# Hybrid attention layer on one core: background transfers without their marks, the heads' values fetched later, the latents' squares three tiles later

## The chip, the core and the metric

The kernel runs on one core of a Trainium2 chip. The core has five engines with instruction streams of their own, which meet only at semaphores: PE (TensorE, matmuls, with its weight loads shown apart as PEld), DVE (VectorE), ACT (ScalarE), POOL (GpSimd) and SP (SyncE). In this kernel SP issues nearly all plain transfers, POOL issues the transfers that add to their target and some stores, and all of them are carried out by the core's 16 DMA engines. The metric is the device time of one execution in microseconds (us), the median over several executions. A measurement of this kernel can tell a change of about 0.5% from none.

## The reference

One decoder layer on 512 tokens of width 2048. The input is normalised and projected; one half of the heads are latent attention heads (MLA, with a rotary part), the other half "forgetting" heads (FoX, whose logits get a running sum of log forget gates). Both are gated, joined, projected back, normalised and added to the input.

```python
def _hybrid_layer(x, cos, sin, g_pre, w_in, g_q, w_uq, g_kv, w_ukv, b_forget, w_out, g_post):
    h = _rms_norm(x, g_pre)
    proj = h @ w_in
    split_points = np.cumsum(IN_SPLITS)[:-1].tolist()
    (q_lat, kv_lat, k_rope_raw, gate_mla,
     fq, fk, fv, f_logit, gate_fox) = jnp.split(proj, split_points, axis=-1)
    o_mla = _mla_branch(q_lat, kv_lat, k_rope_raw, g_q, w_uq, g_kv, w_ukv, cos, sin) * jax.nn.silu(gate_mla)
    o_fox = _fox_branch(fq, fk, fv, f_logit, b_forget) * jax.nn.silu(gate_fox)
    o = jnp.concatenate([o_mla, o_fox], axis=-1) @ w_out
    return x + _rms_norm(o, g_post)
```

Attention is causal, with 8 heads of each kind and 128 columns to a head. Everything is float32.

## The kernel before

**Numbers and matmuls.** Every float32 operand is divided into a high part (a cast on ACT) and a low part (a subtraction on DVE); a product is three matmuls, high by high, high by low and low by high (`mm3`, L148 to L151). Weights come in chunks of 512 KB. `load` issues a chunk's transfer on SP into a tile `raw` (L239 for blocks and sums, L256 for plain columns, L247 for a second addend); `divide` makes `whi` (ACT, L276) and `wlo` (DVE, L279) of it; PE then uses the chunk. `chunk(i)` loads four chunks ahead and divides two ahead. A `raw` tile is one of a few buffers, so a load waits until an earlier chunk's `wlo` is done.

**Stages.** From the start to about 45 us: transposes of x and the first narrow projection (`proj_first`). To 230 us: the value projection `v` and two pairs of FoX gates, in turns with the first q and k. To 420 us: four FoX head pairs (loop at L1253), each a q (`fox_q`), a k (`fox_k`), scores and values. To 600 us: latents (`l`) and MLA gates (`m`). To 725 us: four MLA head pairs. Then the output projection.

**Fewer products, more sums.** The products `v`, `l`, `m` and the output use a scheme of the Strassen-Winograd kind: seven products of half blocks in place of eight, for which blocks of weights are added to or taken from each other first. Some of these sums of weights are made by the DMA engines in the background, through DRAM, and they are the subject here. The list `bg` has 36 of them: `t7` and `t6` for each of `v`, `l` and `m` (four blocks each, 512 KB a block), and `t7`, `t6` and `t4` for the output `o` (four blocks each, 1024 KB a block). A sum takes two transfers: a *first*, a plain copy of one weight block from DRAM to DRAM on SP (L312), and an *accumulate* of the other addend on POOL (L309). The accumulate of a `t6` has the finished `t7` for its addend, that of a `t4` the finished `t6`.

**Steps and marks.** `paced` counts the tiles that PE has been given. Whenever as many have gone by as the pace says (`set_pace`: 4 at first, then 20, 8, 12, 4.9 and so on; double for a wide block), it calls `add_step(n)`, which stands in the program for: the accumulate of sum n-1, the first of sum n, and a *mark* for sum n+1 (L314). The mark is a transfer of 64 bytes on SP, from the `whi` tile that PE is about to use to the first row of the target of sum n+1. The first of sum n+1 overwrites the same bytes, so it must wait for the mark to land, and the mark must wait for the cast of that `whi`. The counter starts at -1, so that sum 0 gets a mark as well.

**Order.** Nothing but a small part at the start is ordered by hand. A planner lists the instructions of each engine; in that list an instruction may stand ahead of one that comes earlier in the program, where the earlier one has something to wait for. Each engine then runs its list strictly in order, and a wait of one holds all behind it. A few instructions are kept in program order (`in_order`).

**Small steps between tiles.** `todo` is a list of small steps. `pump(rate)` runs `rate` of them after each tile of a product, `wait(n)` puts n empty ones in, `drain` runs what is left. Scores, values, divisions of activations and latents all go through it. Of these, three are touched:
- `load_v` (L1130) fetches one head pair's values from DRAM (`v_away`, put there by POOL at the end of the `v` stage) on SP (L1133); `split_v` (L1136) divides them. Before, the fetch stands ahead of the pair's q, and the division ahead of the values of the pair before (for the first pair: at the end of its scores).
- `wait(4)` (L1250) stands ahead of the first pair's scores.
- `latent(i)` (L1306 the square on ACT, L1310 the sum on DVE) for the first four latents, in the product `g5` of `l`, and for the next four in the product `q6` of `m`; the first four read what `lat_less` (L1380) has just written. `lat_sum` is L1376.

Of the kernel before, what the change touches and what calls it, by code (L numbers as in the profile page):

```python
# [12 lines left out]
F32 = mybir.dt.float32  # L13
# [6 lines left out]
P = 128  # L20
D = 2048
S = 512
NT = S // P
# [42 lines left out]
def tile_hybrid_layer(  # L66
# [32 lines left out]
    def slot(name, dt=F32, shape=(P, 2, S)):  # L99

        return sp.tile(list(shape), dt, tag="s", name=name)
# [177 lines left out]
        dve.tensor_tensor(out=lo[:, :m], in0=raw[:, :m], in1=hi[:, :m].bitcast(F32), op=ALU.subtract)  # L279
        ready[i] = [t[:, :m].rearrange("p (k c) -> p k c", k=n) for t in (hi, lo)]  # L280

    state = {"loaded": 0, "divided": 0, "tiles": 0, "step": -1, "pace": 4}

    def prepare(i):
        while state["divided"] < min(len(chunks), i + 1):
# [15 lines left out]
    W, made = {}, {}  # L301
    bg = []

    def add_step(n, mark):


        if n > 0:
            to, _, second = bg[n - 1]
            pool.dma_start(to.rearrange("p (k c) -> p k c", k=2), second, accum_op=ALU.add)  # L309
        if 0 <= n < len(bg):  # L310
            to, first, _ = bg[n]
            nc.sync.dma_start(to.rearrange("p (k c) -> p k c", k=2), first)  # L312
        if n + 1 < len(bg):
            nc.sync.dma_start(bg[n + 1][0][0:1, 0:16], mark)  # L314

    def sum_blocks(g, block, late, width=512):

# [201 lines left out]
    def wait(n):  # L519
        todo.extend([lambda: None] * n)  # L520
# [5 lines left out]
    def set_pace(n):  # L526
        state.update(pace=n, tiles=0)

    def paced(w):

        if state["step"] <= len(bg):
            state["tiles"] += 1
            wide = 0 <= state["step"] < len(bg) and bg[state["step"]][0].shape[1] > 1024
            pace = state["pace"] * (1 + wide)
            if state["tiles"] >= pace:
                state["tiles"] -= pace
                add_step(state["step"], w[0:1, 0, 0:16].bitcast(F32))
                state["step"] += 1

    def proj_T(rng, outs, kh, kl, rate=1):  # L540

        k = 0
        n_k = sum(chunks[i][3] for i in rng)
        for i in rng:
            hi, lo = chunk(i)
            for j in range(chunks[i][3]):
                for o, rows, pick in outs:
                    mm3(o[:rows, :], pick(hi, j), pick(lo, j), kh[k], kl[k], k == 0, k == n_k - 1)
                k += 1
                pump(rate)  # L550
                paced(hi)

    def piece_of(banks, t, width):

# [132 lines left out]
    def enqueue_values(hs):  # L687
        steps = [(h, kb) for h in hs for kb in range(NT)]
        for i in range(len(steps) + 1):
            if i < len(steps):  # L690
                h, kb = steps[i]
                todo.append(lambda h=h, kb=kb: h.flip(kb))
            if i > 0:
                h, kb = steps[i - 1]
                todo.append(lambda h=h, kb=kb: h.values(kb))
# [294 lines left out]
    def product(name, g, parts, o, first, last, rate=1, at=None, held=0, side=(), turned=False):  # L990


        side = deque(side)
        kk = 0

        def step(j, kk, t, hi, lo):
            if not turned:
                mm3(
                    o[t], *parts(kk, t), hi[:, j, :], lo[:, j, :], first and kk == 0, last and kk == 7,
                    skip_group_check=True,  # L1000
                )
                return
            for f in range(2):
                c = slice((2 * t + f) * P, (2 * t + f + 1) * P)
                mm3(
                    o[t][:, f * HALF : (f + 1) * HALF], hi[:, j, c], lo[:, j, c], *parts(kk),
                    first and kk == 0 and f == 0, last and kk == 7, skip_group_check=True,
                )

        rng = list(prods[name, g])  # L1010
        for i in rng[: len(rng) - held]:
            hi, lo = chunk(i)
            for j in range(2):
                if at is not None and kk == at[0]:
                    at[1]()
                for t in range(2):
                    step(j, kk, t, hi, lo)
                kk += 1
                pump(rate)
                paced(hi)  # L1020
                if side and not held and kk % 2 == 0:
                    side.popleft()()
        w = [chunk(i, ahead=0) for i in rng[len(rng) - held :]]
        if w:
            side.popleft()()
        for t in range(2):
            for m in range(2 * len(w)):
                step(m % 2, kk + m, t, *w[m // 2])
            if w:
                finish(t, 2, o[t])  # L1030
# [31 lines left out]
    def fox_k(p, wholes):  # L1062
        kb = [proj_bank(f"fk{p}{i}") for i in range(2)]
        proj_T(fox[p]["k"], [(kb[i], P, two[i]) for i in range(2)], hh, hl)
        k = []
        for i in range(2):
            t = tmp(f"fkt{p}{i}")
            dve.tensor_tensor(out=t, in0=kb[i], in1=rrow, op=ALU.mult)
            k.append(split(t, f"fk{p}{i}"))
            whole_block(wholes, 2 + i, t)  # L1070
        return k
# [55 lines left out]
        for t in range(2):  # L1127
            act.mul(to[:, t, :], o[t], col[:, t0 + t : t0 + t + 1])

    def load_v(pair):  # L1130

        both = slot(f"fv{pair}", shape=(P, NT, 256))
        nc.sync.dma_start(both, v_away[pair].rearrange("p (t c) -> p t c", t=NT))  # L1133
        return both

    def split_v(pair, both):  # L1136

        tiles = v_pair(f"fv{pair}")
        return lambda: values_into(tiles, slice(0, 256), [both[:, t, :] for t in range(NT)], True)
# [107 lines left out]
    v_room.close()  # L1247
    pp = heads_room.enter_context(tc.tile_pool(name="pp", bufs=2, reuse_waits="tile"))
    set_pace(4.9)
    wait(4)  # L1250

    heads = None
    for p in range(4):  # L1253
        vt = load_v(3 - p)
        if p:
            q, wholes = fox_q(p)
            drain()
            keys = [load_keys(2 * (3 - p) + i) for i in range(2)]
            todo.append(split_v(3 - p, vt))
            enqueue_values(heads)  # L1260
            k = fox_k(p, wholes)
            keys = [forget_keys(*a) for a in keys]
            drain()
        else:
            keys = [forget_keys(*a) for a in keys]
            later = split_v(3, vt)
        if p == 2:
            nc.sync.dma_start(gains2[0:6, :], g_q.rearrange("o (k p) -> (o k) p", p=P))
            nc.sync.dma_start(gains2[6:10, :], g_kv.rearrange("o (k p) -> (o k) p", p=P))
            make_gcol(gains2, NK, 10)  # L1270
        vs = values_of(f"fv{3 - p}")
        heads = []
        for i in range(2):
            h = 2 * (3 - p) + i
            heads.append(
                Head(
                    f"f{h}", [q[i]], [k[i]],
                    vs[i],
                    lambda h=h: gates[h],
                    [tuple(wholes[:, 0, c * P : (c + 1) * P] for c in (i, 2 + i))], keys[i],  # L1280
                )
            )
        enqueue_scores(heads, 1)
        if p == 0:
            todo.append(later)
    l4 = slot("l4b", shape=(P, NT, L4))
    nc.sync.dma_start(l4, l4_away.rearrange("p (t c) -> p t c", t=NT))
# [80 lines left out]
    def lat_block(f, half):  # L1368
        return [raws_of[1 + 2 * f + t][:, :, half * HALF : (half + 1) * HALF] for t in range(2)]
# [4 lines left out]
    def lat_sum(to, o, add, op=ALU.add):  # L1374
        for t in range(2):
            dve.tensor_tensor(out=to[t], in0=fold(o[t]), in1=add[t], op=op)  # L1376

    def lat_less(to, o):
        for t in range(2):
            dve.tensor_tensor(out=to[t], in0=to[t], in1=fold(o[t]), op=ALU.subtract)  # L1380
# [65 lines left out]
    product("g7", "l", sums_wide("g7"), C, False, True, side=[*f3[2:], *d3[:2]], turned=True)  # L1446
    lat_sum(lat_block(1, 1), C, pl, ALU.subtract)
    lat_less(lat_block(0, 1), C)
    for i in range(4):
        todo.append(lambda i=i: latent(i, raw(i)))  # L1450
    G = [proj_bank(f"gdl{t}") for t in range(2)]
# [1 line left out]
    lat_sum(lat_block(1, 1), G, lat_block(1, 1))  # L1453
    product("g3", "l", sums_wide("g3"), G, False, True, turned=True)
    lat_sum(lat_block(1, 0), G, lat_block(1, 0))
    for i in range(4, 8):
        todo.append(lambda i=i: latent(i, raw(i)))
    wait(2)
    todo.append(lambda: latent_stats(1))
    for i in range(6):  # L1460
        todo.append(lambda i=i: latent_part(i))
# [29 lines left out]
    for p in range(4):  # L1491
# [31 lines left out]
        for i in c["kv"]:  # L1523
            hi, lo = chunk(i)
            for j in range(chunks[i][3]):
                fst, lst = kk == 0, kk == KVR // P - 1
                for n in range(2):
                    w = cols(256 * n)
                    mm3(kb[n], w(hi, j), w(lo, j), knh[kk], knl[kk], fst, lst)
                for t in range(NT):  # L1530
                    o = vb[t // 2][:, (t % 2) * 256 : (t % 2) * 256 + 256]
                    ts = slice(t * P, (t + 1) * P)
                    mm3(
                        o, knh[kk][:, ts], knl[kk][:, ts], v_cols(hi, j), v_cols(lo, j),
                        fst and t % 2 == 0, lst, skip_group_check=True,
                    )
                kk += 1
                pump(2)
                paced(hi)
        k = [[split(kb[i], f"mk{p}{i}"), (kr, None)] for i in range(2)]  # L1540
        kw = [[whole_block(wholes, 2 + i, kb[i]), kr.bitcast(F32)[:, :P]] for i in range(2)]
        drain()
# [231 lines left out]
```

## Time and profile before

| What | Value |
|---|---|
| Times of three runs | 902.98, 903.35 and 906.58 us, median 903.35 us |
| Profiled execution | 903.03 us, of which the span from the first instruction to the last is 901.3 us |
| Granted TensorE clock | 0.997 of full speed |
| PE busy | 885.5 us |
| DVE, ACT and POOL busy | 678.0, 454.2 and 66.0 us |
| Moved by the DMA engines | 218.26 MB, mean 242 GB/s |

The profile is one execution. A matmul of 512 columns is shown as some 390 ns long but the next one starts after some 230 ns, since they are pipelined; so a busy share of PE near 100% says that it was never without work, not that nothing could go faster. In the views, "SPq" is the transfer queue of SP, a bracket after a row gives the idle time of the engine ahead of the instruction and what ended it, and "xN" counts instructions.

### The profile page before, as it was taken

To read this page: it belongs to the slowest core of one execution; us is meant where nothing else is said; L and a number is where in the kernel's file an instruction comes from. 1 tells how busy PE (TensorE), PEld (TensorE's weight loads), DVE (VectorE), ACT (ScalarE), POOL (GpSimd) and SP (SyncE) were. 2 spreads that over 40 slices of the span, in tenths; PEclk is the share of its full clock that TensorE was granted. 3 is DMA by queue.
4 is the path that set the end of the run, shared out by engine and by line. 5 is a ranking of instruction groups with operands and counts; after the bars stand their busy time and mean duration, and the time that the engine had idled before them with its cause. 6 is when DMAs were issued, how large, how long until landed. Compare 5 with 4: busy or idle time off the path is not lost.

```text
span 901.3 us, 12830 instructions
## 1 busy us (share of the span) xinstructions
PE 885.5 (98%) x4594; PEld 755.4 (84%) x4594; DVE 678.0 (75%) x1120; ACT 454.2 (50%) x837; POOL 66.0 (7%) x86
## 2 busy tenths in 40 slices
PE   8999999999999999999999999999999999999997
PEld 8988887888878888888998998788888888877885
DVE  4579995658775738667588897867978895988786
ACT  6944443334243423435545565535554676646383
POOL 1010110011211101000000000000000000000021
PEclk9999999999999999999999999999999999999998
DMA  9798799799999999896799986788862136799878
GB/s 288 229 267 241 223 317 304 223 238 305 259 282 279 243 244 240 212 271 153 276 398 393 331 293 169 152 211 196 220 149 79 62 119 212 232 324 306 278 214 253
DMA packets 125515, 218.26 MB, mean 242 GB/s; under 512 B 16362, under 2 KB 53764, under 8 KB 124428
## 3 DMA queue, kind: packets, MB, share of 16 engines
q1 hardware_dynamic: 113340, 179.41, 61.0%
q0 software_dynamic: 11376, 37.75, 21.0%
q8 instruction: 36, 0.59, 0.3%
q10 hardware_dynamic: 736, 0.29, 0.1%
q14 instruction: 27, 0.22, 0.1%
HBM read 202.72 MB, written 65.03 MB: 297 GB/s over the span
## 4 chain that ended last, share of the span: by engine, by line
PE 74%; DVE 14%; DMA 6%; issue 3%; ACT 3%; SPq 0%; ACTq 0%; DVEq 0%
DVE wlo L279 4%; PE in L583 3%; PE fk L151 3%; PE fk L149 3%; PE fk L150 3%; PE fq L149 3%; PE fq L151 3%; PE fq L150 3%; PE sm L626 2%; PE mq L149 2%; PE mq L151 2%; PE mq L150 2%; ACT whi L276 1%; PE oa L149 1%; PE od L150 1%
## 5 line engine op out<-in xcount | busy, mean ns | idle before, releaser
L279 DVE TENSOR_TENSOR wlo<-raw,whi 128x1024 fp32r<-128x1024 f32 (+3 forms) x217 | 256.7, 1187 | 128.9 <-ACT whi L276 119.7
L276 ACT CAST whi<-raw 128x1024 fp32r<-128x1024 f32 (+3 forms) x217 | 221.2, 1023 | 256.8 <-issue 34.8
L149 PE MATMUL fk<-h,whi 128*128 128x512 f32 x128 | 52.4, 410 | 0.0
L149 PE MATMUL fq<-h,whi 128*128 128x512 f32 x128 | 50.8, 397 | 0.0
L149 PE MATMUL fg<-h,whi 128*128 128x512 f32 x128 | 50.3, 393 | 0.0
L151 PE MATMUL fk<-h,wlo 128*128 128x512 f32 x128 | 50.2, 392 | 0.0
L150 PE MATMUL fk<-h,whi 128*128 128x512 f32 x128 | 50.1, 391 | 0.0
L151 PE MATMUL fq<-h,wlo 128*128 128x512 f32 x128 | 50.0, 390 | 0.0
L150 PE MATMUL fq<-h,whi 128*128 128x512 f32 x128 | 49.9, 390 | 0.0
L151 PE MATMUL fg<-h,wlo 128*128 128x512 f32 x128 | 49.9, 390 | 0.0
L150 PE MATMUL fg<-h,whi 128*128 128x512 f32 x128 | 49.9, 390 | 0.0
L266 DVE TENSOR_TENSOR raw<-raw,second 128x1024 f32<-128x1024 f32 x32 | 39.0, 1217 | 0.8 <-DMA second<-in_w_out_dram 0.8
L648 ACT ACTIVATE pf<-sf,stf 128x128 f32<-128x128 f32 (+3 forms) x32 | 16.7, 523 | 30.0 <-DVE stf L641 30.0
L583 PE MATMUL in<-whi,h 128*128 128x328 f32 x128 | 29.7, 321 | 0.0
L149 PE MATMUL mq<-ln,whi 128*128 128x512 f32 x72 | 28.8, 400 | 0.0
L151 PEld LDWEIGHTS fk<-h,wlo 128*128 128x128 f32 x128 | 24.0, 188 | 5.3
L151 PEld LDWEIGHTS fq<-h,wlo 128*128 128x128 f32 x128 | 24.0, 188 | 5.3
L151 PEld LDWEIGHTS fg<-h,wlo 128*128 128x128 f32 x128 | 24.0, 188 | 5.1
L150 PE MATMUL mq<-ln,whi 128*128 128x512 f32 x72 | 28.3, 392 | 0.0
L151 PE MATMUL mq<-ln,wlo 128*128 128x512 f32 x72 | 28.2, 391 | 0.0
L150 PEld LDWEIGHTS fg<-h,whi 128*128 128x128 f32 x128 | 24.1, 188 | 4.7
L149 PEld LDWEIGHTS fg<-h,whi 128*128 128x128 f32 x128 | 24.0, 188 | 4.7
(558 smaller groups left out, 2465.4 us busy)
## 6 DMA issues: line engine op xcount, KB each, us to landing
raw<-in_w_in_dram SPq DMA_DIRECT2D x96, 512.0 KB
raw<-in_w_out_dram SPq DMA_DIRECT2D x32, 512.0 KB
second<-in_w_in_dram SPq DMA_DIRECT2D x24, 512.0 KB
bmg<-awaymg SPq DMA_DIRECT2D x20, 256.0 KB
awaymg<-rmg POOLq DMA_DIRECT2D x8, 512.0 KB, 7.9
raw<-t6v SPq DMA_DIRECT2D x8, 512.0 KB
t7o<-in_w_out_dram SPq DMA_DIRECT2D x4, 1024.0 KB
t7o<-in_w_out_dram POOLq DMA_DIRECT2D x4, 1024.0 KB, 10.5
```

The lines of the kernel that those rows point to most:

```text
L149: pe.matmul(o, ah, bh, start=first, stop=False, **kw)
L150: pe.matmul(o, ah, bl, start=False, stop=False, **kw)
L151: pe.matmul(o, al, bh, start=False, stop=last, **kw)
L266: tc.keep_in_program_order(dve.tensor_tensor(out=raw, in0=raw, in1=second, op=ALU.add))
L276: cast = act.copy(hi[:, :m], raw[:, :m])
L279: dve.tensor_tensor(out=lo[:, :m], in0=raw[:, :m], in1=hi[:, :m].bitcast(F32), op=ALU.subtract)
L583: pe.matmul(banks[t][:, :n], a[k][:, tss[t]], b[:, j, :], start=k == 0 and m == 0, stop=k == NK - 1 and m == 2,)
L626: pe.matmul(s[:, :nn], a[:, qs], c[:, :nn], start=(i == 0), stop=(i == len(pairs) - 1))
L648: act.activation(p, s[:, :n], AF.Exp, bias=st[:, 0:1], scale=unit, accum_out=st[:, 1:2])
```

## The change

The marks go: `add_step` no longer issues them, `paced` no longer hands a tile over, and the counter starts at 0. The values of the first FoX pair are fetched by a step placed twelfth in the list that runs in the next q; those of the others are fetched after the pair's q and keys and divided after the values of the pair before. The four empty steps ahead of the first scores become two. Three empty steps are put ahead of each group of four latents, and the two ahead of `latent_stats(1)` become one.

```diff
-    state = {"loaded": 0, "divided": 0, "tiles": 0, "step": -1, "pace": 4}
+    state = {"loaded": 0, "divided": 0, "tiles": 0, "step": 0, "pace": 4}
...
-    def add_step(n, mark):
+    def add_step(n):
...
         if 0 <= n < len(bg):
             to, first, _ = bg[n]
             nc.sync.dma_start(to.rearrange("p (k c) -> p k c", k=2), first)
-        if n + 1 < len(bg):
-            nc.sync.dma_start(bg[n + 1][0][0:1, 0:16], mark)
...
-    def paced(w):
+    def paced():
...
-                add_step(state["step"], w[0:1, 0, 0:16].bitcast(F32))
+                add_step(state["step"])
...
-    def load_v(pair):
+    def load_v(pair, both=None):
-        both = slot(f"fv{pair}", shape=(P, NT, 256))
+        both = both or slot(f"fv{pair}", shape=(P, NT, 256))
...
     set_pace(4.9)
-    wait(4)
+    wait(2)
     heads = None
     for p in range(4):
-        vt = load_v(3 - p)
         if p:
             q, wholes = fox_q(p)
             drain()
             keys = [load_keys(2 * (3 - p) + i) for i in range(2)]
-            todo.append(split_v(3 - p, vt))
+            vt = load_v(3 - p)
             enqueue_values(heads)
+            todo.insert(10, split_v(3 - p, vt))
             k = fox_k(p, wholes)
...
         else:
             keys = [forget_keys(*a) for a in keys]
-            later = split_v(3, vt)
+            first_v = slot("fv3", shape=(P, NT, 256))
+            later = split_v(3, first_v)
...
         enqueue_scores(heads, 1)
         if p == 0:
+            todo.insert(12, lambda: load_v(3, first_v))
             todo.append(later)
...
     lat_less(lat_block(0, 1), C)
+    wait(3)
     for i in range(4):
         todo.append(lambda i=i: latent(i, raw(i)))
...
     lat_sum(lat_block(1, 0), G, lat_block(1, 0))
+    wait(3)
     for i in range(4, 8):
         todo.append(lambda i=i: latent(i, raw(i)))
-    wait(2)
+    wait(1)
     todo.append(lambda: latent_stats(1))
```

More of the change, by code (lines that the diff above doesn't have):

```diff
@@ L550, in proj_T @@
                 pump(rate)
-                paced(hi)
+                paced()
     def piece_of(banks, t, width):
@@ L1019, in product @@
                 pump(rate)
-                paced(hi)
+                paced()
                 if side and not held and kk % 2 == 0:
@@ L1538, in tile_hybrid_layer @@
                 pump(2)
-                paced(hi)
+                paced()
         k = [[split(kb[i], f"mk{p}{i}"), (kr, None)] for i in range(2)]
```

## The prediction

> **What bounds the kernel now.** I read the page first, then what PE waits for, then the transfer queue of SP in order of time. The profiled execution took 903.03 us: the span below and 1.7 us around it. It stands 0.3 us under the median of the three runs, 903.35 us, so its terms can be set against that median as they are. A measurement of this kernel tells about 0.5%, 4.5 us, from no change.
>
> ```profile
> span 901.3 us, 12830 instructions
> ...
> PE 885.5 (98%) x4594; PEld 755.4 (84%) x4594; DVE 678.0 (75%) x1120; ACT 454.2 (50%) x837; POOL 66.0 (7%) x86
> ```
>
> PE is without work for 901.3 - 885.5 = 15.8 us in all. The four waits that this change could reach are in the view of waits, PE alone:
>
> ```profile
> PE sm L626 <- ACT pm L648: 1.3, 1, 1.3
> ...
> PE gdl L149 <- DVE lat L1376: 1.1, 1, 1.1
> PE ptf L657 <- ACT pf L648: 1.1, 1, 1.1
> ...
> PE sf L626 <- ACT pf L648: 0.4, 1, 0.4
> ```
>
> Each is a single wait, 3.9 us together. So whatever the edits do for PE's waits is worth at most 3.9 us, and the question is what they may break: PE's feed. How full the DMA engines are that feed it is in the view of windows (the last two columns are their busy share and GB/s; the second stretch holds little but one 1024 KB first, the third little but its accumulate):
>
> ```profile
> 45.00:230.00 185.00, 184.14 (x815) 151.58 (x814) 142.96 (x184) 77.96 (x98) 20.83 (x25) 1.00 0.90 263
> 562.00:566.00 4.00, 3.90 (x18) 2.77 (x16) 3.89 (x10) 0.91 (x4) 0.00 (x0) 1.00 0.66 151
> 568.00:576.00 8.00, 7.38 (x31) 5.30 (x30) 7.29 (x15) 5.46 (x8) 0.00 (x0) 1.00 0.97 171
> ```
>
> From 45 to 230 us they are busy for 0.90 of the time; 0.10 x 185 = 18.5 us is free. At full share a first moves 151 / 0.66 = 229 GB/s, an accumulate 171 / 0.97 = 176 GB/s.
>
> **The marks: what holds a first in its place?** The planner may put a transfer ahead of earlier ones that have to wait. SP's queue shows how far this goes:
>
> ```profile
> 19.50 0.95 SPq L247 DMA_DIRECT2D second<-in_w_in_dram  x2
> 20.49 0.36 SPq L1268 DMA_DIRECT2D gains<-in_g_q_latent_dram  x1
> 21.68 0.27 SPq L1269 DMA_DIRECT2D gains<-in_g_kv_latent_dram  x1
> ```
>
> L1268 and L1269 stand in the third round of the loop over FoX pairs, work that PE reaches after 300 us. They read an input, wait for nothing of their stage, and go out at 20 us, when SP's earlier loads have to wait for buffers. The `second` loads belong to the first chunks that have two addends, whose own `raw` loads, the first of line L239, go out at 105.71 us (below). And a first leaves when its own mark allows it, not when its step comes:
>
> ```profile
> 105.71 3.31 SPq L239 DMA_DIRECT2D raw<-in_w_in_dram  x2
> 109.08 0.32 SPq L314 DMA_DIRECT2D t6v<-whi  x1
> 111.33 0.37 SPq L239 DMA_DIRECT2D raw<-in_w_in_dram  x1
> 112.19 0.57 SPq L312 DMA_DIRECT2D t6v<-in_w_in_dram  x1
> ...
> 141.35 0.28 SPq L314 DMA_DIRECT2D t7v<-whi  x1
> ```
>
> In the program the first at 112.19 stands directly ahead of the mark at 141.35, one whole step behind its own mark at 109.08. It went 3 us behind its own mark, past the loads between. A first reads weights and writes a DRAM tile of its own; without the mark it waits for nothing. I therefore expect all 36 firsts to move to where the `gains` went, about 17 to 45 us, at 0.57 us of issue each, 36 x 0.57 = 20.5 us, ahead of or between the loads that PE needs from 30 us on. By the trace of before, how many were out by 230 us (all instructions of line L312 in that window):
>
> ```profile
> L312 SPq DMA_DIRECT2D t7v<-in_w_in_dram x4: 564/708/1312, 41.8 to 145.1; - x4
> L312 SPq DMA_DIRECT2D t6v<-in_w_in_dram x4: 563/566/568, 46.2 to 150.6; - x4
> L312 SPq DMA_DIRECT2D t7l<-in_w_in_dram x3: 563/573/1324, 173.6 to 226.5; - x3
> L312 SPq DMA_DIRECT2D t6l<-in_w_in_dram x2: 564/564/564, 179.9 to 213.7; - x2
> ```
>
> Thirteen. Moved forward are 23: 11 of 512 KB and 12 of 1024 KB, 17.5 MiB or 18.35 MB. At 229 GB/s that is **80 us** of all DMA engines, of which 18.5 us fall into free time: **+61.5 us**, if the accumulates all stayed where they are. They won't all: each can go once its first has landed. Before, 12 are issued by 230 us (one step behind the firsts); the other 24 are 18 MiB or 18.9 MB, at 176 GB/s **107 us**. The ends for them are 0 and 107 us. No row decides between these: in the rows of before accumulates follow their firsts, which speaks for 107, but those of `o` can run after 230 us, where their own firsts no longer are. I take half, **+53.5 us**, and keep both ends.
>
> That PE can't hide this follows from how one load fares behind one first:
>
> ```profile
> 613.07 0.56 SPq L312 DMA_DIRECT2D t7o<-in_w_out_dram  x1
> 613.72 1.07 SPq L256 DMA_DIRECT2D raw<-in_w_ukv_dram  x2
> ```
>
> ```profile
> 623.02 1.05 ACT L276 CAST whi<-raw 128x1024 fp32r<-128x1024 f32 x1 [2.30 <-DMA raw<-in_w_ukv_dram]
> ```
>
> Issued right behind one first, the load is there 9.3 us later, and ACT waits 2.3 us for it; PE's wait `sm` of 1.3 us follows from this. Chunks are loaded four ahead. PE's starts lie 0.23 us apart with 512 columns and 0.12 us with 256:
>
> ```profile
> 244.02 0.39 PE L150 MATMUL fq<-h,whi 128*128 128x512 f32 x1
> 244.25 0.39 PE L151 MATMUL fq<-h,wlo 128*128 128x512 f32 x1
> ```
>
> ```profile
> 537.94 0.28 PE L150 MATMUL gdl<-bmg,whi 128*128 128x256 f32 x1
> 538.06 0.28 PE L151 MATMUL gdl<-bmg,wlo 128*128 128x256 f32 x1
> ```
>
> A chunk of a block product is 12 matmuls, 2.8 us, so four cover 11 us, and not 25 MB of firsts. Late in the kernel the background is then over and the load at 613.72 has nothing ahead of it: PE's 1.3 us should go, **-1.3 us**; 0 if something else holds that cast.
>
> What else goes with the marks: 36 issues on SP of about 0.3 us (the rows of L314), and SP's waits for their casts:
>
> ```profile
> SPq L314 <- ACT whi L276: 74.4, 24, 10.6
> ...
> SPq L1133 <- DMA v_away<-vo: 10.0, 2, 8.6
> ```
>
> The 74.4 us are worth nothing by themselves: the next load behind a mark waits for a buffer that a later chunk's `wlo` frees, so it would wait anyway. The counter's start at 0 moves each step one step earlier; next to the firsts' own move that is nothing.
>
> **The values' fetch.** Before, the fetch L1133 holds SP for 8.6 us until the values have been stored. Behind it three marks bunch up, the first at 246.00, and a cast that needs the `whi` buffer that this mark reads waits for it to land:
>
> ```profile
> 246.00 0.36 SPq L314 DMA_DIRECT2D t7l<-whi  x1
> ```
>
> ```profile
> 251.98 1.05 ACT L276 CAST whi<-raw 128x1024 fp32r<-128x1024 f32 x1 [5.47 <-DMA t7l<-whi]
> ```
>
> ACT stands for 5.47 us, its exponentials come late, and PE waits for them twice, `sf` 0.4 and `ptf` 1.1 us. Either edit alone, no mark or no early fetch, removes that: **-1.5 us**. The first scores come two tiles earlier, so one more of them runs inside the q and one less at its drained end: hidden behind the q's matmuls, 0. Added is no instruction; the fetch now stands twelve tiles of 6 x 0.23 = 1.4 us into the q, its division behind the last score, some five tiles or 7 us later; if it lands after that, PE's first values wait for it. What is queued behind the division is ACT's next cast of a chunk, which PE needs two chunks on. The other pairs' fetches have the 14 us of ten tiles before their division, and the scores and exponentials of the q as cover. Both at 0; the rows of a load behind a first (9.3 us) make this part -1.5 to +2 us.
>
> **The squares.** Before, ACT waits 2.59 us with the first square:
>
> ```profile
> 530.43 0.63 ACT L1306 ACTIVATE ls<-lat 128x512 f32<-128x512 f32 x1 [2.59 <-DVE lat L1380]
> ```
>
> ```profile
> 536.38 2.35 DVE L279 TENSOR_TENSOR wlo<-raw,whi 128x1024 fp32r<-128x1024 f32 x2
> 538.65 1.28 DVE L1376 TENSOR_TENSOR lat<-gdl,lat 128x512 f32<-128x512 f32 x2
> ```
>
> The squares move 3 tiles of 12 x 0.12 = 1.4 us, 4.3 us, past that wait. But PE's own wait here, `gdl` 1.1 us, is for a DVE that works without a gap until 538.65, on two `wlo` last; the same sums are still ahead of it. The second four and all behind them, `latent_stats` too, move two steps on, one tile at two steps a tile, beside the products of `m`, and still end within them. Between -1.1 and +1.1 us I take 0.
>
> **Sum.** 903.0 + 61.5 + 53.5 - 1.3 - 1.5 = **1015 us**, with 960 (no accumulate moves) and 1069 (all move) as its ends.
>
> **Rivals.**
> (a) *The accumulates take their full turn.* Then all 107 us fall into the stretch: 903.0 + 61.5 + 107 - 2.8 = **1069 us**. For it: POOL is nearly idle (66.0 us busy) and issues as soon as a first lands. Against it: a `t6` needs its `t7` landed. [...]
> (b) *The loads keep going first.* If the planner puts the firsts only into gaps between loads, over the first 200 us, they use the 18.5 us of free time and delay loads by what is in flight. A quarter of the forecast's 115 us: **some 930 us**. For it: a load that is ready stands earlier in the program.
> (c) *The firsts stay in their steps*, not slower: place, SP's list between 17 and 45 us; it decides as long as no more moves than free time takes, about one transfer in seven (18.5 of 80 + 53.5 us). Then the marks' and the fetch's waits go and nothing is lost: 903.0 - 1.5 - 1.3 = **900 us**, 899 with the squares' 1.1. For it: steps and paces are in the program. Against it: the rows at 20.49 and 112.19.
> (d) *The fetch moves no later in fact*, since the planner may pull it ahead as well: 1.5 us more than each of these.
>
> **Chances.** Forecast 0.56 (its own range 960 to 1060), (a) 0.12, (b) 0.15, (c) 0.17; (d) changes none. Slower by over 0.5%: the forecast, (a), 0.13 of (b), 0.02 of (c): 0.83. Within 0.5%: 0.02 of (b), 0.11 of (c): 0.13. Faster by over 0.5% needs all four waits and one more us: 0.04. Cases of 0.3 lie below 960, so the range has to take them in: 899 to 1069 leaves out the lower edge of (c) and the upper half of (a), and some at the forecast's upper end.
>
> **What would show it.** Right: L312 rows all between 17 and 100 us in place of 41.8 to 647.1; PE waits of many us ahead of the first projections, ended by `whi`, `wlo` or a DMA; a DMA share near 1 in the stretched first part and a low one from 300 us on; PE's busy time still near 885 us. The `t7l<-whi` row and the 5.47 us are gone either way. Wrong: L312 rows spread over 600 us as before. Then it is (c). The size is wrong if the first part ends much before 330 us.

## The result, and the profile after

| | us, median | runs | lowest to highest |
|---|---|---|---|
| Before | 903.16 | 6 | 901.43 to 906.58 |
| After | 1020.71 | 6 | 1018.20 to 1022.00 |

The changed kernel takes 1.130 times as long (95% interval 1.1277 to 1.1329): **117.6 us slower**. The prediction was 1015 us, with a range of 899 to 1069. The profiled execution of after took 1021.18 us.

First the page of after: span and busy times, then PE, its granted clock and the DMA share in 40 slices of 25.5 us.

```profile
span 1019.4 us, 12723 instructions
...
PE 913.4 (90%) x4594; PEld 768.1 (75%) x4594; DVE 678.2 (67%) x1120; ACT 454.5 (45%) x837; POOL 64.5 (6%) x86
...
PE   9768773734979999999999999999999999999997
...
PEclk9989885876989999999999999999999999999999
DMA  9999999999996752424334998832213314779878
```

All the loss stands in the first twelve slices, some 300 us. There the DMA engines are full and PE is not; from then on PE is full and the DMA engines have time to spare. The bytes are the same 218.26 MB in both pages. Next, the firsts (the transfers of line L312 by target: issue time in ns, then the first and the last start in us):

```profile
L312 SPq DMA_DIRECT2D t7v<-in_w_in_dram x4: 558/644/5847, 17.8 to 38.6; - x4
...
L312 SPq DMA_DIRECT2D t6m<-in_w_in_dram x4: 580/3260/6792, 80.0 to 113.5; - x4
...
L312 SPq DMA_DIRECT2D t4o<-in_w_out_dram x4: 1027/2930/6056, 132.0 to 270.2; - x4
```

Before, the first of them started at 41.8 and the last at 647.1 us. Now they run from 17.8 to 270.2 us. SP's queue in order of time shows them going out ahead of a load of weights:

```profile
17.81 0.67 SPq L312 DMA_DIRECT2D t7v<-in_w_in_dram  x1
18.53 1.07 SPq L312 DMA_DIRECT2D t6v<-in_w_in_dram  x1
19.64 0.62 SPq L312 DMA_DIRECT2D t7v<-in_w_in_dram  x1
20.69 0.55 SPq L312 DMA_DIRECT2D t6v<-in_w_in_dram  x1
21.34 1.30 SPq L256 DMA_DIRECT2D raw<-in_w_in_dram  x2
```

The accumulates (L309) follow. Of the last of them, those of `t4o`, the kernel before issued four between 362.2 and 655.9 us:

```profile
L309 POOL DMA_DIRECT2D t4o<-t6o x4: 799/808/866, 192.1 to 295.2; - x4
```

What PE waits for (total us, times, longest), and then, of all engines, what those casts wait for:

```profile
PE vg L149 <- ACT whi L276: 29.3, 2, 14.7
PE fg L149 <- ACT whi L276: 17.7, 4, 6.8
PE fg L151 <- DVE wlo L279: 17.4, 4, 12.8
PE rrow L505 <- issue: 7.9, 1, 7.9
PE va L150 <- DVE wlo L279: 6.9, 4, 3.3
```

```profile
ACT whi L276 <- DMA raw<-in_w_in_dram: 130.6, 28, 11.0
```

PE waits for casts, and the casts for loads of weights (130.6 us in all, where the kernel before shows 1.3). The large waits stand in the first gates (`fg`) and the `v` products (`va`, `vg`), not later. Only for the wait at `rrow`, 63.7 us from the start, does the profile name no releaser.

**Where the time went, stage by stage.** The best measure for this is the start of the same matmul in both kernels. The first start of the last group of products in `v` (tile `vc`), and of the first latents (`gl`), before and then after:

```profile
L149 PE MATMUL vc<-whi,bmq x16: 389/389/474, 197.2 to 207.5; 128*128 128x512 f32 x16
L149 PE MATMUL gl<-h,whi x64: 278/283/365, 419.3 to 459.1; 128*128 128x256 f32 x64
```

```profile
L149 PE MATMUL vc<-whi,bmq x16: 389/389/477, 316.8 to 327.1; 128*128 128x512 f32 x16
L149 PE MATMUL gl<-h,whi x64: 277/283/365, 537.1 to 576.9; 128*128 128x256 f32 x64
```

At `vc` the changed kernel is 119.6 us late, at `gl` 117.8 and at the end 118.1 (1019.4 - 901.3). So 119.6 us are lost by the end of the `v` stage and 1.8 us come back in the FoX heads. What lies behind `gl` changes 0.3 us in all.

**What the DMA engines did until `vc`.** The window up to that matmul (DMA share and GB/s are the last columns), and the two queues' bytes and share of the 16 engines' time in it; q1 carries SP's transfers, q0 POOL's. Before:

```profile
0.00:197.20 197.20, 194.08 (x956) 166.50 (x956) 140.20 (x201) 98.15 (x184) 20.81 (x35) 1.00 0.88 259
```

```profile
q1 hardware_dynamic: 30494, 40.20, 63.6%
q0 software_dynamic: 3636, 10.69, 24.3%
```

After:

```profile
0.00:316.80 316.80, 222.42 (x956) 179.56 (x956) 140.89 (x201) 98.19 (x184) 44.45 (x60) 0.85 1.02 286
```

```profile
q1 hardware_dynamic: 37412, 60.11, 56.6%
q0 software_dynamic: 8688, 30.41, 45.5%
```

PE has done the same 956 matmuls in both windows. SP's queue took 0.636 x 197.2 = 125.4 us of all engines before and 0.566 x 316.8 = 179.3 us after: **54 us** more for 19.9 MB more, 370 GB/s. POOL's took 47.9 and then 144.1 us: **96 us** more for 19.7 MB, 205 GB/s. That is 150 us of added transfer time. 0.12 x 197.2 = 24 us were free before, and the share of 1.02 after gives 6 more: 150 - 30 = 120 us, the delay at `vc`. This sum must close, since it is share times length of the two windows put in another way. What it shows is that the engines were full all through and which queue took the added time; whether bytes moved early set the delay is tested below. Those rates are quotients of this window, not properties of one transfer.

### The profile page after: what moved, and what is told of

It is laid out like the page before. It is cut to its first block, busy times and chain, and to the rows that moved or that the text cites. A ratio compares the mean times of both kernels' runs of the same rounds, so it can differ in the third digit from the quotient of the medians.

```text
span 1019.4 us, 12723 instructions
## 1 busy us (share of the span) xinstructions
PE 913.4 (90%) x4594; PEld 768.1 (75%) x4594; DVE 678.2 (67%) x1120; ACT 454.5 (45%) x837; POOL 64.5 (6%) x86
## 2 busy tenths in 40 slices
DMA packets 125443, 218.26 MB, mean 214 GB/s; under 512 B 16290, under 2 KB 53692, under 8 KB 124356
## 3 DMA queue, kind: packets, MB, share of 16 engines
q1 hardware_dynamic: 113268, 179.41, 53.5%
## 4 chain that ended last, share of the span: by engine, by line
PE 63%; DMA 10%; issue 6%; DVE 4%; ACT 2%; POOL 1%; SPq 0%; ACTq 0%; DVEq 0%; POOLq 0%
DMA raw<-in_w_in_dram 5%; PE fk L149 3%; PE fk L151 3%; DMA awaymg<-rmg 3%; PE fk L150 3%; PE sm L624 2%; PE fq L149 2%; PE fq L151 2%; PE fq L150 2%; DVE wlo L279 2%; PE mq L149 2%; PE mq L151 2%; PE mq L150 2%; PE oa L149 1%; PE oa L151 1%
## 5 line engine op out<-in xcount | busy, mean ns | idle before, releaser
L276 ACT CAST whi<-raw 128x1024 fp32r<-128x1024 f32 (+3 forms) x217 | 221.1, 1022 | 353.6 <-DMA raw<-in_w_in_dram 130.6
L149 PE MATMUL fg<-h,whi 128*128 128x512 f32 x128 | 55.6, 434 | 17.7 <-ACT whi L276 17.7
L151 PE MATMUL fg<-h,wlo 128*128 128x512 f32 x128 | 54.9, 429 | 17.5 <-DVE wlo L279 17.4
L149 PE MATMUL fk<-h,whi 128*128 128x512 f32 x128 | 53.8, 420 | 4.0 <-ACT whi L276 4.0
L150 PE MATMUL fg<-h,whi 128*128 128x512 f32 x128 | 54.2, 423 | 0.0
L150 PE MATMUL fk<-h,whi 128*128 128x512 f32 x128 | 51.1, 399 | 0.0
L149 PE MATMUL fq<-h,whi 128*128 128x512 f32 x128 | 50.8, 397 | 0.0
L150 PE MATMUL fq<-h,whi 128*128 128x512 f32 x128 | 49.9, 390 | 0.0
L151 PEld LDWEIGHTS fg<-h,wlo 128*128 128x128 f32 x128 | 26.6, 207 | 26.7 <-DVE wlo L279 20.8
L149 PEld LDWEIGHTS fg<-h,whi 128*128 128x128 f32 x128 | 26.8, 209 | 24.6 <-ACT whi L276 19.4
L149 PE MATMUL vg<-whi,smg 128*128 128x512 f32 x16 | 8.0, 500 | 29.3 <-ACT whi L276 29.3
L1593 POOL DMA_DIRECT2D c<-in_x_dram x8 | 7.0, 990 | 409.8 <-ACT c L1592 409.8
L149 PEld LDWEIGHTS fk<-h,whi 128*128 128x128 f32 x128 | 24.7, 193 | 9.0 <-ACT whi L276 4.4
L150 PEld LDWEIGHTS fg<-h,whi 128*128 128x128 f32 x128 | 26.9, 210 | 5.6
L1038 DVE TENSOR_TENSOR xr<-h 128x512 f32<-128x512 f32 x16 | 10.5, 684 | 27.7 <-DMA awaymg<-rmg 27.7
```

What stands on the lines that cost most here:

```text
L149: pe.matmul(o, ah, bh, start=first, stop=False, **kw)
L150: pe.matmul(o, ah, bl, start=False, stop=False, **kw)
L151: pe.matmul(o, al, bh, start=False, stop=last, **kw)
L276: cast = act.copy(hi[:, :m], raw[:, :m])
L1038: dve.tensor_tensor(out=pair[h][:, i, :], in0=hh[k].bitcast(F32), in1=hl[k].bitcast(F32), op=ALU.add)
L1593: pool.dma_start(to, x[piece(t, c)], accum_op=ALU.add)
```

## The experiments

Every ratio below is to the kernel before, run beside it; the interval is that of 95%.

### Which edit does it: marks, fetch or squares

Four kernels carry only some of the edits. The marks alone:

```diff
-        if n + 1 < len(bg):
-            nc.sync.dma_start(bg[n + 1][0][0:1, 0:16], mark)
...
-    state = {"loaded": 0, "divided": 0, "tiles": 0, "step": -1, "pace": 4}
+    state = {"loaded": 0, "divided": 0, "tiles": 0, "step": 0, "pace": 4}
```

> Before with the marks taken out and the counter started at 0, nothing else. If the marks alone are the cause, this takes what the whole change takes plus the 1.5 us that the later fetch would have saved, and that saving comes with the marks' going too: 1016 to 1024 us. If the fetch or the squares have a share in the 117 us, it lies below by that share, say under 1005 us.

The fetch alone:

```diff
-    wait(4)
+    wait(2)
...
-        vt = load_v(3 - p)
         if p:
...
+            vt = load_v(3 - p)
             enqueue_values(heads)
+            todo.insert(10, split_v(3 - p, vt))
...
+            todo.insert(12, lambda: load_v(3, first_v))
```

> Before with the values' fetch and division moved and two empty steps fewer, marks kept. Expected: the 5.47 us cast wait behind the mark at 246 us goes and with it PE's two waits of 0.4 and 1.1 us, so 901.7 us against 903.2, ratio 0.998. Rival: the values come late and PE waits for them, 904 to 906 us.

The squares alone:

```diff
     lat_less(lat_block(0, 1), C)
+    wait(3)
...
+    wait(3)
     for i in range(4, 8):
         todo.append(lambda i=i: latent(i, raw(i)))
-    wait(2)
+    wait(1)
```

> Before with the three empty steps ahead of each group of latents only. Expected: no change within 1 us, 902 to 904 us, since PE's wait there is for a DVE that is busy without a gap. Rival: the square's 2.59 us on ACT had been passed on to PE, then 900 to 902 us.

Fetch and squares, with the marks kept:

> Before with the moved fetch and the moved squares, marks kept: the change without its first part. Expected: the sum of the two alone, 901 to 903 us, ratio 0.997 to 1.000. If the two edits need each other, outside of that.

| Edits | us | ratio | interval |
|---|---|---|---|
| marks out | 1016.93 | 1.1274 | 1.1255 to 1.1293 |
| fetch | 899.73 | 0.9974 | 0.9963 to 0.9985 |
| squares | 903.75 | 1.0015 | 1.0001 to 1.0028 |
| fetch and squares | 902.08 | 0.9999 | 0.9986 to 1.0011 |

Taking the marks out makes the whole loss. The fetch by itself gains 2.3 us (1.4 to 3.3 by the interval), and the squares by themselves cost about 1.3 us (0.1 to 2.5); together they come to nothing that can be measured.

The fetch's gain did not come by a later fetch. SP's queue before, and then with the fetch moved:

```profile
243.10 2.07 SPq L1133 DMA_DIRECT2D fv<-v_away  x2
```

```profile
234.21 0.72 SPq L314 DMA_DIRECT2D t7l<-whi  x1
242.87 0.33 SPq L1133 DMA_DIRECT2D fv<-v_away  x1
```

The first pair's fetch goes out when it did, and SP still stands 7.8 us for the stored values. But one mark, at 246.00 us in the kernel before, now goes ahead of that wait, and the cast that waited 5.47 us for it no longer does. The fetches of the other pairs do go out 12 us and more later.

PE's waits with the squares moved show where their cost may lie. Before, the wait for `lat` was 1.1 us, `gdm` waited 0.2 us at L149, and `gcm` waited 0.4 us for another operand.

```profile
PE gdl L149 <- DVE lat L1376: 1.6, 1, 1.6
...
PE gdm L150 <- DVE wlo L279: 0.7, 1, 0.7
...
PE gcm L149 <- DVE latk_y L1329: 0.4, 1, 0.4
```

2.7 us in place of 1.7: 1.0 us more. One execution can't prove a microsecond, and this one spans 901.3 us like that of before. But the three waits of 1.6, 0.7 and 0.4 us stand in six of the seven profiles with the squares moved (the seventh starves in that stretch), and in none without. That the full change came out 3.8 us over the marks alone, where fetch and squares together measure nothing, stays open. By the two profiles 4.8 us of difference stand ahead of `vc` (316.8 and 312.0 us), where neither the fetch nor the squares have come yet; the two intervals overlap, and the two kernels were not run side by side.

### Is it the missing mark, or the lost order?

If the marks matter because they hold each first in its place, a first that is held there by the planner's own rule must do as well. In the changed kernel:

```diff
-            nc.sync.dma_start(to.rearrange("p (k c) -> p k c", k=2), first)
+            tc.keep_in_program_order(nc.sync.dma_start(to.rearrange("p (k c) -> p k c", k=2), first))
```

> The changed kernel, no marks, with each first kept in its place in the program on SP. If what costs is that the firsts move forward, and not that the marks are gone, the time is that of before without the marks and with the moved fetch and squares: 899 to 903 us. If the marks do something else that the kernel needs (spacing in time, one at a time), it stays well above, 910 us and more.

901.62 us, 0.9983 (0.9970 to 0.9996). With no mark in the program the loss is gone. L312 in its trace:

```profile
L312 SPq DMA_DIRECT2D t6v<-in_w_in_dram x4: 563/627/718, 21.2 to 144.4; - x4
...
L312 SPq DMA_DIRECT2D t4o<-in_w_out_dram x4: 563/564/687, 358.2 to 679.3; - x4
```

So it is the lost order that costs the time. The same pin with the fetch moved and the squares left where they were:

> Before with no marks, each first kept in its place in the program on SP, and the moved fetch; the squares as before. If a mark costs nothing by itself once the fetch no longer bunches them, this is the fetch alone with marks: ratio 0.9960 to 0.9985, 899 to 901 us. If the 36 small transfers and SP's waits for them cost something, below 0.9960. If the squares' edit is what held the pinned kernel back, it lies under that one's 0.9983.

899.77 us, 0.9969 (0.9958 to 0.9980), the same as the fetch alone with its marks. A mark by itself costs nothing that can be measured: the 74.4 us for which SP waited with marks were hidden. This version and the fetch alone are the two fastest that make all the sums, 0.3% under the kernel before.

### What the early transfers cost: firsts or accumulates?

First, both orders without any background accumulate:

```diff
-        if n > 0:
-            to, _, second = bg[n - 1]
-            pool.dma_start(to.rearrange("p (k c) -> p k c", k=2), second, accum_op=ALU.add)
```

In the changed kernel:

> The changed kernel without the accumulates of the background (the sums of weights then lack their second addend). If the loss is the DMA engines' time: the firsts alone, 25 brought forward, 19.4 MB at 229 GB/s or 85 us; free time is 24 us plus the 31 us that before's own eleven accumulates took there: 30 us more than the same kernel with marks, 925 to 945 us. If the accumulates on POOL's queue are the cause, this is within 5 us of the same kernel with marks.

In the kernel before:

> Before without the accumulates of the background (as above), marks kept: the other side of the comparison. PE is the limit there, so 900 to 903 us.

913.06 us (1.0108, 1.0072 to 1.0144) and 898.40 us (0.9947, 0.9930 to 0.9964): early firsts alone cost 14.7 us, half of what was expected. 9.8 of them are lost by `vc`; the rest may in part be the fetch and the squares, in which the two kernels differ as well. The windows up to the first `vc` matmul, in the changed order and in the old one:

```profile
0.00:207.10 207.10, 199.45 (x956) 169.57 (x956) 140.32 (x201) 98.17 (x184) 9.01 (x24) 0.99 0.92 316
```

```profile
0.00:197.30 197.30, 194.57 (x956) 166.64 (x956) 140.03 (x201) 98.17 (x184) 9.01 (x24) 1.00 0.73 234
```

316 x 207.1 less 234 x 197.3 is 19.3 MB more, in 0.92 x 207.1 less 0.73 x 197.3 = 46.5 us of transfer time: some 415 GB/s, not the 229 GB/s of one lone first. And without accumulates 0.27 x 197.3 = 53 us are free there. So the firsts would fit into them; that the 9.8 us are the moments at which they stand ahead of a load is not shown. The second kernel also tells that the accumulates cost the kernel before 4.8 us.

Then the changed kernel with its firsts free, and each accumulate kept in program order on POOL:

```diff
-            pool.dma_start(to.rearrange("p (k c) -> p k c", k=2), second, accum_op=ALU.add)
+            tc.keep_in_program_order(pool.dma_start(to.rearrange("p (k c) -> p k c", k=2), second, accum_op=ALU.add))
```

> The changed kernel with each accumulate kept in its place in the program on POOL: the firsts come forward, the sums do not. Counted in DMA time by queue up to the end of the v stage: firsts 54 us more than before, free time 24 us, so about 30 us more, 933 us (920 to 945). If the two don't add up so, and firsts are dear only beside sums, under 915 us; if firsts alone were the price, over 990 us.

958.36 us, 1.0611 (1.0592 to 1.0630): 25 us over the expected 933. Up to `vc` it was as expected, 223.5 us in place of 197.2, +26.3. But this kernel loses a second time. Two windows of it, and PE's waits there:

```profile
480.00:520.00 40.00, 34.05 (x203) 29.86 (x203) 23.04 (x24) 14.81 (x18) 4.83 (x6) 0.96 1.04 330
520.00:560.00 40.00, 26.05 (x146) 22.35 (x144) 20.64 (x22) 11.40 (x14) 3.57 (x4) 0.83 1.04 307
```

```profile
PE gdm L150 <- DVE wlo L279: 14.5, 3, 10.2
...
PE gbm L150 <- DVE wlo L279: 8.5, 2, 5.6
```

The accumulates of the output's sums went out up to 559.3 us, into the products of `l` and `m`, which load two addends a chunk. In the kernel before the accumulates leave that stretch empty, none between 408.66 and 566.43 us. A DMA share over 1 does not tell by itself that PE starves: the kernel before, in the latents and without accumulates, has it as high while PE is full.

```profile
440.00:480.00 40.00, 40.00 (x268) 37.09 (x267) 29.30 (x29) 20.25 (x24) 1.61 (x3) 1.00 1.04 400
```

The engines moved 400 GB/s there, and 307 to 330 beside the accumulates. The expectation had counted only the first stretch. The second cost more: this kernel is 24.5 us late at the first `gl` matmul (443.8 us) and 54.4 us late at the first `gdl` (581.1 and 526.7 us), and from 480 to 580 us DVE waits 31.6 us for loads of second addends. So the moved transfers were not dear at the start alone.

### Part of the sums moved early

The 36 sums are 24 of 512 KB a block (`v`, `l`, `m`) and 12 of 1024 KB (`o`), 12.6 MB of firsts each. With marks only for the twelve of `o`:

```diff
-        if n + 1 < len(bg):
+        if 24 <= n + 1 < len(bg):
```

> Before with marks kept only for the 12 wide sums of the output; the 24 sums of 512 KB have none. If the loss is the DMA engines' time for what is brought forward, less some 24 us of free time: by the point where the v stage ends, 13 firsts and some 13 accumulates of 0.52 MB more than before, 13.6 MB at 259 GB/s or 53 us, less 24: about 29 us more than before, 932 us (925 to 945). If the loss comes from the accumulates that block POOL's queue, it is nearly as large as with all of them out, 980 us and more, since the queue is as full through the first 150 us.

955.88 us, 1.0579 (1.0548 to 1.0610), between the two answers: neither was right, and the count has to be made at the point that is worst off. At the first matmul of `vg` PE is 186.2 - 130.5 = 55.7 us late. The windows up to it, in the kernel before and here:

```profile
0.00:130.50 130.50, 128.13 (x664) 112.20 (x665) 102.04 (x157) 72.74 (x151) 15.56 (x30) 1.00 0.88 256
```

```profile
0.00:186.20 186.20, 143.09 (x663) 119.84 (x664) 103.85 (x158) 72.73 (x151) 33.21 (x48) 0.88 1.01 287
200.00:250.00 50.00, 50.00 (x222) 41.39 (x221) 25.23 (x30) 17.50 (x24) 0.00 (x0) 1.00 0.47 143
```

By then 24 firsts and 24 accumulates are out in place of 6 and 6: 9.4 MB more of each. At the rates of after that is 9.4 / 0.370 = 25 and 9.4 / 0.205 = 46 us, less 0.12 x 130.5 = 16 free: 55 us. This was worked out after the result. Then the share falls to 0.47, but PE is full as well and can't win anything back. Free time behind the tight point is worth nothing to it.

The mirror of this, with marks for the 24 narrow sums alone (`if n + 1 < 24:`):

> The kernel before, with its marks kept for the 24 narrow sums and taken away for the 12 wide output sums alone, the mirror of e6_o_marked. The theory counts DMA time up to the end of the v stage: 24 transfers of 0.52 MB, 12.6 MB, come early as firsts at about 370 GB/s (34 us) and 12.6 MB as sums at about 205 GB/s (61 us), less some 24 us that the DMA has free there before: 70 us, so about 973 us, 955 to 990. If the bytes moved early do not set it (the firsts being cheap, or the narrow sums being what stops the first projections), it stays below 945; if late sums are more than their bytes cost, it is over 1000.

983.40 us, 1.0898 (1.0858 to 1.0937), inside the expected 955 to 990. Its queues up to `vc` (279.4 us):

```profile
q1 hardware_dynamic: 33755, 52.77, 57.8%
q0 software_dynamic: 5992, 23.51, 40.3%
```

SP's queue took 36 us more than before for 12.6 MB, POOL's 65 us more for 12.8 MB: 101 us less the free 24 leaves 77, and the start of `vc` was 82.2 us late. The two halves cost 52.7 and 81.7 us; together they would be 134, 20 us more than the 114 of all marks taken out. Free time can't be the reason: each half by itself uses the same 24 free us, so that their sum would come out smaller, not larger. With the narrow sums early, the engines were busy for only 0.47 of the time from 200 to 250 us, which the wide transfers may fill when all are early. That was not tested.

### POOL's queue

In the changed kernel the stores of finished rows (`awaymg`, L932) stand in POOL's list among accumulates. The chain of work that ended last, between 135 and 260 us of after (start, us, what):

```profile
158.45 21.38 issue
179.85 0.52 POOL t6o L309
...
180.41 0.47 POOL awaymg L932
...
180.97 14.71 DMA awaymg<-rmg
```

A store waits 21.4 us behind an accumulate that itself waits for its addend, the accumulate of `t7o` issued at 156.65 us, to land. The store then lands 14.7 us after it was issued. The changed kernel with those stores issued by SP:

```diff
-            pool.dma_start(to.rearrange("p (h c) -> p h c", c=HALF), src)
+            nc.sync.dma_start(to.rearrange("p (h c) -> p h c", c=HALF), src)
```

> The changed kernel with the puts of the activations' sums (line L932) issued by SP, so that they no longer stand behind accumulates on POOL. If the DMA engines' time for what is brought forward is the whole price, it stays: 1012 to 1028 us. If the puts that POOL issues late are a cause of their own (the first at 156 us where it was 81 us before), it falls to 1000 us or less.

1002.49 us, 1.1089 (1.1067 to 1.1112), in the gap between the two answers: 18 us of the 118 go. By the rates above, the stores' 4.2 MB would be 11 us on SP's queue in place of 20 on POOL's. But the 205 GB/s of POOL's queue is that of accumulates. In the changed kernel without accumulates, POOL's queue up to `vc` (207.1 us) holds stores alone:

```profile
q0 software_dynamic: 1456, 5.24, 6.2%
```

That is 5.24 MB in 12.8 us, 410 GB/s: by itself POOL's queue isn't dear for a store. So the stores' place behind the accumulates, as the chain has it, may be all of the 18 us; this kernel changes place and queue at once, and how the two divide stays open. The larger part of the loss does not hang on where these stores stand: 100 of the 118 us stay, with a DMA share of 1.05 up to 297 us.

## Why the prediction was right

**The mechanism held.** The firsts went ahead in SP's list, past loads that had to wait, and took the feed of the first projections. The marks alone give the loss, and an order without marks takes it away. PE's waits came in the first projections, ended by `whi` and `wlo`, as was written. One sign was off: not all firsts go out between 17 and 45 us, nor by 100. Eight are out by 45 us, 22 by 100, and the last goes at 270.2 us. SP's list has loads between them that wait for buffers, and an issue itself now takes up to 9.6 us (`t7o`), where 0.57 was usual. All are out ahead of the end of the `v` stage, and so they count in full in the sum.

**Three terms of the sum were off, and cancelled.**

| Term | Predicted, us | Measured, us | From |
|---|---|---|---|
| firsts' transfer time | 80 | 54 | queue q1 up to `vc` |
| free time of the DMA engines | -18.5 | -30 | share 0.88, then 1.02 |
| accumulates' transfer time | 53.5 | 96 | queue q0 up to `vc` |
| sum at the end of `v` | 115 | 120 | starts of `vc`: 119.6 |

That 1015 us came so near to 1020.71 was luck: the firsts were put 26 us too high, the free time 11.5 us and the accumulates 42.5 us too low. (The lower end, 960, is 961.7 us by its own terms.) The measured terms close by construction, as said above; where they were used for a time ahead of its run, they gave 30 for 26.3 us (firsts alone) and 70 for 82.2 us (wide sums alone) at `vc`.

The step "at full share a first moves 151 / 0.66 = 229 GB/s" failed. It took the share of one transfer that runs nearly alone for its price in company, and its window caught only the tail of that copy, which was issued at 558.92 us: from 556 to 566 us SP's queue moved 1.22 MB in 46.6% of the time, 262 GB/s. Some 370 GB/s was the price in after, 415 without accumulates. The firsts alone cost +26.3 us up to `vc` when measured by themselves, where the term said +61.5. And "I take half" failed: all of those accumulates fell into the stretch (96 us, as they went at 205 rather than 176 GB/s). So rival (a) was right that all of them move, and only the oversized firsts made its time, 1069, too long. With the firsts at 54 us and 30 free, its own sum would be 903.0 + 24 + 96 - 2.8 = 1020. Up to `vc`, POOL's queue had 45.5% and SP's 56.6% of the engines' time. No run here shows how an engine divides its time between the two queues, nor that both were full all the time.

**The small terms.** The fetch was put at -1.5, with -1.5 to +2 as its ends; alone it measured -2.3 us. "Either edit alone" held: from `vc` to `gl` it is 222.1 us before, 220.3 with the fetch alone, 220.1 with the marks out alone, and 220.3 after. The way was another than forecast, as the first pair's fetch did not go out later. The wait `sm` (-1.3) is gone from the list of after. It is gone as well where every mark was kept and only the fetch or only the squares were moved, in the latter with a first at 612.80 us as in the kernel before; so that first was not shown to be its cause. The squares were put at 0 between -1.1 and +1.1; they measured +1.3, whose interval reaches below 1.1. PE's waits in `l` and `m`, 1.0 us longer, speak against "the same sums are still ahead of it" (`gdl`, 1.1 to 1.6 us) and "still end within them" (`gdm` 0.7 us at L150).

**The rivals.** (c), firsts stay, fell with the rows of L312. (b), loads first, had it right that the firsts go out between loads over some 250 us, but they did not keep to free time, and its 930 us fell. (d), that the fetch moves no later, was right for the first pair by the rows at 243.10 and 242.87; its price of 1.5 us fell, since the wait went all the same.

**PE's busy time** was to stay near 885 us and came to 913.4; the next but one section has the reason.

## What to carry to other kernels

A transfer that looks like dead weight may be what holds a large one in its place: before a dependency is taken away, ask what the planner may then pull forward, and whether the DMA engines have room there. Price a moved transfer in the company that it will have (bytes and share of its queue in a full window: 370 GB/s here), not by a lone one (taken as 229 GB/s), and count at the point where PE first runs out of work, as free time later paid nothing back (a DMA share of 0.47 beside a PE busy for 50.00 of 50 us). If an order is wanted, state it as an order: the pinned kernels lost nothing by it (0.9983 and 0.9969).

## What the runs showed of the hardware

**The granted clock was lower where PE starved.** Three windows of after (PE's busy time comes first, the granted clock stands third from the end):

```profile
150.00:200.00 50.00, 25.89 (x89) 19.06 (x89) 15.19 (x22) 6.97 (x9) 7.27 (x9) 0.73 1.03 286
200.00:250.00 50.00, 19.49 (x60) 14.01 (x60) 17.26 (x21) 10.53 (x12) 7.43 (x10) 0.64 1.02 277
...
400.00:500.00 100.00, 100.00 (x480) 83.00 (x479) 65.23 (x145) 36.48 (x81) 2.73 (x4) 1.00 0.37 110
```

60 matmuls take 19.5 us at a clock of 0.64, and 480 take 100 us at 1.00. From 248.94 to 251.50 us of after, matmuls of 512 columns start 0.43 us apart (clock 0.52 from 248 to 252 us), where at 244 us of before they start 0.23 us apart. Up to `vc` the same 956 matmuls are busy for 222.42 us at a mean clock of 0.85, in place of 194.08 at 1.00, which is all of the 27.9 us by which PE's busy time grew. PE had nothing to do in the rest of that time, so the lower clock there need not have cost anything; it was not tested by itself. What the rows do show is that busy time isn't work done: PE's "90%" in the page of after holds 28 us more than before for the same 4594 matmuls.

**Equal bytes, unequal time.** Up to `vc` 19.7 MB of accumulates took 96 us and 19.9 MB of copies 54, both from DRAM to DRAM: by these queues' time an accumulated byte was 1.8 times as dear as a copied one. It is not POOL's queue as such: without accumulates that queue moved its stores at 410 GB/s.
